# The head of a hybrid decoder step: TensorE's order written out tile by tile, one Newton chain, first weights in three pieces, and a constant table loaded last

## The chip, the cores and the metric

One Trainium2 chip, of which the kernel uses one core. The core has five engines that run their own instruction streams side by side: TensorE (PE in the profile, with its weight loads as PEld), VectorE (DVE), ScalarE (ACT), GpSimd (POOL) and SyncE (SP, which only issues transfers here). Transfers between the chip's memory (HBM) and the on-chip memory (SBUF) run on 16 DMA engines. The metric is the device time of one execution in microseconds, the median of several runs.

## The reference

One inference step of a decoder layer with two branches. The part that the change touches is the layer's beginning, for 1024 prompt tokens and 8 x 4 sample tokens (1056 rows in all, model width 1024):

```
mod = silu(c) @ w_ada + b_ada                 # c: 1 prompt and 8 sample vectors
shift, scale, gate = split(mod, 3)
r = rsqrt(mean(x * x) + EPS)
h = x * r * g_norm * (1 + scale) + shift
u = h @ w_in                                  # then split into queries, keys, values, gates, index rows
...
s = einsum(q_idx, k_idx); relu; weighted sum  # index scores, causal mask, top 256 keys per token
```

After it come the index scores and the choice of 256 keys, sparse attention over the chosen keys, a retention (linear attention) branch, gates, two output projections, a final projection and a norm. None of that is changed.

## The kernel before

Everything in this text happens in the **head**, the first 60 us. `h` is held turned, as eight tiles `k = 0..7` of 128 model channels by 1056 tokens.

- **x blocks** (`x_block`). The x rows are loaded in nine blocks (32 sample rows, then eight blocks of 128 prompt rows). TensorE turns each block into PSUM, ScalarE and VectorE each copy half of it to `XT`, and one of them sums the squares of the rows (VectorE for the blocks listed in `SQD`).
- **Norms** (`norms`). VectorE computes 1/sqrt by Newton steps (`rsqrt`), TensorE spreads the factors over 128 partitions, and a copy leaves them in `RB`.
- **Modulation** (`modulation`). For each `k`, TensorE multiplies the conditioning vectors `scT` with two 512 KB column blocks of `w_ada` (line 212), ScalarE copies the result (`ar`), TensorE turns it, and VectorE reduces it to `cm`, which holds shift and scale of the 128 channels.
- **Tile** (`h_tile`). ScalarE forms the factors `AA` and `BB` (lines 337 and 338), VectorE scales the tile (line 340) and applies the sample rows' own factors (lines 342, 345, 346), ScalarE writes the rounded high part `hh` in two halves (line 348), VectorE the remainder `hl` in two halves (line 349).
- **First products** (`start_two`). The first two 128-column blocks of `w_in` are split into high and low parts `W` and multiplied with all tiles: for each `k` three terms (high weights x `hh`, high x `hl`, low x `hh`), each of five matmuls of 352 or 400 columns, 120 in all, at line 235.

Two more things matter. `C` is a table of constants: its first 128 columns (the identity) are loaded first of all, and the other 664 columns, with a causal mask from column `C_CAUS` on, in one transfer at line 362. The mask is first read by two small VectorE instructions of the index stage, which fill the first blocks of the selection mask `bi`:

```
for b in (0, 1):
    nc.vector.tensor_scalar(BI[b][:, b * 128:], C[:, C_CAUS:C_CAUS + 128], 1.0e30 / 3.0e38, None, op0=OP.mult)
```

They stand far down in the source, but nothing that they need comes from the stages between.

**What sets the order.** Each engine executes its instructions in one fixed order. A scheduler sets that order when the kernel is built, by a timeline of its own; `tc.issue_after(x)` keeps an instruction behind `x`, and `tc.high_priority()` prefers what is inside. So instructions of a later stage can land between those of the head, as the two `bi` instructions do. SyncE issues the loads in its own order, and they are served on one queue.

The functions that the change touches, with the line numbers of the profile:

Of the kernel before, what the change touches and what calls it, by code (L numbers as in the profile page):

```python
# [8 lines left out]
F32 = mybir.dt.float32  # L9
# [4 lines left out]
OP = mybir.AluOpType  # L14
# [4 lines left out]
D = 1024  # L19
# [10 lines left out]
EPS = 1e-6  # L30
SQD = (1, 4)
SEQ = (8, 0, 1, 2, 3, 4, 5, 6, 7)
# [85 lines left out]
def _hybrid_step(ctx, tc, A, outs, dbg):  # L118
# [11 lines left out]
    ps1 = ExitStack()  # L130
    ps = ps1.enter_context(tc.tile_pool(name="ps", bufs=1, reuse_waits="tile", space=PSUM))
    psj_ = ExitStack()
# [92 lines left out]

    def start_two(W):

        x, y = pl(), pl()
        parts_ = [(p[:, :sl.stop - sl.start], sl, i) for p, sl, i in
                  zip((pj(), pj(), x[:, :512], x[:, 512:], y[:, :512]), chunks + late, (0, 0, 0, 1, 1))]  # L230

        line = [(0, 0), (0, 1), (1, 0), (1, 1), (0, 2), (1, 2)] + [(k, term) for k in range(2, KT) for term in range(3)]
        for n, (k, term) in enumerate(line):
            for p, sl, i in parts_:
                nc.tensor.matmul(p, W[i][term == 2][:, k], (HL if term == 1 else HH)[k][:, sl],
                                 start=(n == 0), stop=(n == len(line) - 1))
        return [p for p, sl, i in parts_]

    scT = cst.tile([128, KT, 32], F32, name="scT")
    xp, xs = A["x_prompt"][0], A["x_sample"].rearrange("b i d -> (b i) d")  # L240
    with ExitStack() as s0:
# [5 lines left out]
        part = lambda: sp.tile([128, D], F32, name="x", bufs=11)  # L247
        craw, th = [part()[:9] for _ in (0, 1)]
        nc.scalar.dma_start(craw[0:1], A["c_prompt"])
        nc.scalar.dma_start(craw[1:9], A["c_sample"])  # L250
        rows = sp.tile([48, 128], F32, name="rows")
# [17 lines left out]
        def cond():  # L269
            nc.scalar.activation(th, craw, AF.Tanh, scale=0.5)  # L270
            nc.vector.scalar_tensor_tensor(th, th, 1.0, craw, op0=OP.add, op1=OP.mult)
            pc = pt()
            for k in range(KT):
                nc.tensor.transpose(pc[:, k * 16:k * 16 + 9], th[:, k * 128:k * 128 + 128], ident[:9, :9])
            nc.vector.memset(scT, 0.0)
            nc.scalar.activation(scT[:, :, :9], pc[:, :KT * 16].rearrange("p (k c) -> p k c", c=16)[:, :, :9],
                                 AF.Copy, scale=0.5)
# [7 lines left out]
        def x_block(i):  # L285

            t = SEQ[i]
            n, x = size(t), X[t]
            p = pl().rearrange("p (k t) -> p k t", k=KT)
            for k in range(KT):  # L290
                nc.tensor.transpose(p[:, k, :n], x[:n, 128 * k:128 * k + 128], ident[:n, :n])
# [6 lines left out]
            for g, copy in ((slice(0, 4), nc.scalar.copy), (slice(4, 8), nc.vector.tensor_copy)):  # L298
                copy(XT[:, g, t * 128:t * 128 + n], p[:, g, :n])

        def norms(i0, i1):

            with tc.high_priority():
                v = sp.tile([128, i1 - i0], F32, name="vv", bufs=2)
                nc.vector.tensor_scalar(v, ssq[:, i0:i1], 1.0 / D, EPS, op0=OP.mult, op1=OP.add)
                r = rsqrt(sp, v, i1 - i0)
                newton = nc.cur_bb.bb.instructions[-1]
                p, c0 = pj(), 128 * SEQ[i1 - 4]
                for i in range(i1 - 4, i1):
                    o = 128 * (i - i1 + 4)  # L310
                    last = nc.tensor.matmul(p[:, o:o + 128], r[:, i - i0:i - i0 + 1].to_broadcast([128, 128]), ident, start=True, stop=True)
                nc.scalar.copy(RB[:, c0:c0 + 512], p)
            if i0 == 0:
                p = pt()
                nc.tensor.matmul(p[:, :NS], r[:NS, 0:1].to_broadcast([NS, 128]), ident[:NS, :NS], start=True, stop=True)
                nc.vector.tensor_tensor(XT[:, :, T:], XT[:, :, T:], p[:, :NS].unsqueeze(1).to_broadcast([128, KT, NS]), op=OP.mult)
            return last.ins, newton

        def modulation(k):

            pm = pt()
            for o in (0, 1):
                ada_rows(pm[:, 128 * o:128 * o + 128], lambda c: wa[k][o][:, c])
            ar = sp.tile([128, 256], F32, name="ar", bufs=2)
            nc.scalar.copy(ar, pm[:, :256])
            pm = pt()
            for o in (0, 1):
                turned = nc.tensor.transpose(pm[:, 128 * o:128 * o + 128], ar[:, 128 * o:128 * o + 128], ident)

            cm = sp.tile([128, 2, 9], F32, name="cm", bufs=2)  # L330
            nc.vector.tensor_reduce(cm, pm[:, :256].rearrange("p (o q r) -> p o r q", o=2, q=4)[:, :, :9], op=OP.add, axis=AX.X)
            return cm.rearrange("p o r -> p (o r)"), turned.ins

        def h_tile(k, pm):
# [4 lines left out]
            h = XT[:, k]  # L339
            scaled = nc.vector.scalar_tensor_tensor(h[:, :T], h[:, :T], AA[:, k, 0:1], RB[:, :T], op0=OP.mult, op1=OP.mult)  # L340

# [4 lines left out]
            nc.vector.tensor_tensor(hs, hs, by_seq(BB), op=OP.add)  # L346
            for sl in (slice(0, 528), slice(528, TT)):
                high = nc.scalar.activation(HH[k][:, sl], h[:, sl], AF.Identity, bias=shift)
                rest = nc.vector.scalar_tensor_tensor(HL[k][:, sl], h[:, sl], shift, f32(HH[k][:, sl]), op0=OP.add, op1=OP.subtract)
            return high, rest, moved, scaled  # L350

        wa, loads = {}, []

        def load_wa(k):

            wa[k] = [part().rearrange("p (k f) -> p k f", f=128) for _ in (0, 1)]
            for o, w in enumerate(wa[k]):
                loads.append(nc.sync.dma_start(w, wcols(A["w_ada"][0], KT, 1024 * o + 128 * k, 128)))

        for t in SEQ:  # L360
            x_load(t)
        nc.sync.dma_start(C[:, C_CAUS:], A["cst"][:, C_CAUS:])
# [6 lines left out]
        W, ws = [], []  # L369
        zeros = sp.tile([128, 512], BF, name="zeros")  # L370
        nc.vector.memset(zeros, 0.0)

        def idle_products(n, behind):

            x = pl()
            with tc.issue_after(behind):
                for i in range(n):
                    nc.tensor.matmul(x[:, 512 * (i % 2):512 * (i % 2) + 512], zeros[:, :128], zeros, start=True, stop=True)

        W = [[sp.tile([128, KT, 128], F32R, name="w", bufs=4) for _ in "hl"] for _ in (0, 1)]  # L380
        rounded, rest = lambda i: nc.scalar.copy(W[i][0], ws[i]), lambda i: nc.vector.tensor_sub(W[i][1], ws[i], f32(W[i][0]))
        ends = []
        load_wa(0)
        for k in range(KT):
            if k + 1 < KT:
                load_wa(k + 1)
            if k == 0:
                with tc.issue_after(loads[-1].ins):
                    ws = [wload(wp, w_in, f, 128) for f in (O_KI, O_QI)]
                pm, turned = modulation(k)  # L390
                idle_products(8, turned)
            else:
                with tc.issue_after(spread):
                    pm, turned = modulation(k)
            ends.append(h_tile(k, pm))
            if k == 0:
                for i in (0, 1):
                    with tc.issue_after(ends[0][0 if i else 2].ins):
                        rounded(i)
            if k == 1:  # L400
                for i in (0, 1):
                    with tc.issue_after(ends[1][1 if i else 3].ins):
                        rest(i)
        head_ends = ends[-1]
        first = start_two(W)


# [1107 lines left out]
```

## Time and profile before

| what | value |
|---|---|
| median of 3 runs | 1106.63 us (1106.52 to 1106.79) |
| the profiled execution's own time | 1106.86 us |
| span of its instructions | 1105.1 us |
| granted TensorE clock | 0.998 |
| busy over the span | PE 98%, DVE 61%, ACT 43%, POOL 21% |
| first product of the head (line 235) | starts at 27.04 us |
| last product of the head | starts within the group at 60.28 us; TensorE goes on to line 773 at 60.62 us |

In a row of the timeline the first number is the start in us from the span's beginning, the second the duration, then engine, line, operation, output <- inputs with shapes, the count, and in brackets how long the engine sat idle before it and what ended that. A row of stages gives busy us of each engine and its instructions, the granted clock, the mean busy share of the 16 DMA engines and GB/s.

### The profile page before, as it was taken

To read this page: it belongs to the slowest core of one execution; us is meant where nothing else is said; L and a number is where in the kernel's file an instruction comes from. 1 tells how busy PE (TensorE), PEld (TensorE's weight loads), DVE (VectorE), ACT (ScalarE), POOL (GpSimd) and SP (SyncE) were. 2 spreads that over 40 slices of the span, in tenths; PEclk is the share of its full clock that TensorE was granted. 3 is DMA by queue.
4 is the path that set the end of the run, shared out by engine and by line. 5 is a ranking of instruction groups with operands and counts; after the bars stand their busy time and mean duration, and the time that the engine had idled before them with its cause. 6 is when DMAs were issued, how large, how long until landed. Compare 5 with 4: busy or idle time off the path is not lost. (4 is left out here: it accounts for less than half of the span.)

```text
span 1105.1 us, 20498 instructions
## 1 busy us (share of the span) xinstructions
PE 1078.5 (98%) x8138; PEld 982.2 (89%) x8138; DVE 679.3 (61%) x1646; ACT 471.8 (43%) x916; POOL 229.5 (21%) x195
## 2 busy tenths in 40 slices
PE   6999999999999999999999999999999999999997
PEld 5789899899999989999899999887998888898776
DVE  6876359698877878999122222210357767497765
ACT  6574445554654555332243333311336666343211
POOL 0003016013311221020422222244114333100000
PEclk9999999999999999999999999999999999999999
DMA  9923334264244515532877768486798520367431
GB/s 312 244 72 106 114 110 144 56 212 136 79 144 132 168 42 187 150 87 96 286 246 231 232 186 234 131 285 237 243 326 300 176 75 30 120 201 255 157 120 58
DMA packets 156023, 185.63 MB, mean 168 GB/s; under 512 B 18629, under 2 KB 126989, under 8 KB 154838
## 3 DMA queue, kind: packets, MB, share of 16 engines
q1 hardware_dynamic: 145632, 147.80, 42.7%
q0 software_dynamic: 9856, 35.66, 9.8%
q8 instruction: 64, 1.05, 0.4%
q10 hardware_dynamic: 438, 0.86, 0.2%
q14 instruction: 33, 0.27, 0.1%
HBM read 139.33 MB, written 41.17 MB: 163 GB/s over the span
## 5 line engine op out<-in xcount | busy, mean ns | idle before, releaser
L218 PE MATMUL pj<-hh,wh 128*128 128x352 f32 (+1 forms) x1168 | 383.5, 328 | 1.0 <-ACT raw L720 0.8
L219 PE MATMUL pj<-hl,wh 128*128 128x352 f32 (+1 forms) x1168 | 378.8, 324 | 0.0
L220 PE MATMUL pj<-hh,wl 128*128 128x352 f32 (+1 forms) x1168 | 377.4, 323 | 0.0
L218 PEld LDWEIGHTS pj<-hh,wh 128*128 128x128 f32 x1168 | 219.3, 188 | 10.5 <-issue 7.5
L219 PEld LDWEIGHTS pj<-hl,wh 128*128 128x128 f32 x1168 | 219.7, 188 | 5.0 <-issue 4.4
L220 PEld LDWEIGHTS pj<-hh,wl 128*128 128x128 f32 x1168 | 219.5, 188 | 3.5 <-issue 3.2
L882 DVE TENSOR_SCALAR_CACHE_REDUCE eq<-sc,cand 128x896 bf16<-128x896 f32 (+4 forms) x155 | 135.7, 875 | 2.5
L204 ACT CAST wh<-ws 128x1024 fp32r<-128x1024 f32 (+1 forms) x65 | 61.0, 942 | 111.4 <-PE pj L219 82.3
L205 DVE TENSOR_TENSOR wl<-ws,wh 128x1024 fp32r<-128x1024 f32 (+1 forms) x47 | 52.6, 1122 | 35.7 <-ACT wh L204 35.4
L205 POOL TENSOR_TENSOR wl<-ws,wh 128x1024 fp32r<-128x1024 f32 x18 | 43.1, 2394 | 147.6 <-ACT wh L204 147.6
L1229 POOL TENSOR_SCALAR lg<-lg,st 128x1024 f32<-128x1024 f32 (+7 forms) x64 | 47.6, 752 | 115.5 <-DVE st L1228 58.7
L1099 DVE COPY kt<-str 128x512 f32<-128x512 f32 x32 | 22.1, 690 | 64.3 <-PE str L1097 60.6
L1227 ACT ACTIVATE lg<-lg,st 128x1024 f32<-128x1024 f32 (+7 forms) x64 | 49.4, 774 | 27.6 <-DVE st L1226 26.0
L1426 PE MATMUL pj<-woh,MH 128*128 128x512 f32 (+1 forms) x136 | 51.4, 378 | 0.0
L1427 PE MATMUL pj<-wol,MH 128*128 128x512 f32 (+1 forms) x136 | 51.2, 377 | 0.0
L1428 PE MATMUL pj<-woh,ML 128*128 128x512 f32 (+1 forms) x136 | 51.2, 376 | 0.0
L1066 POOL DMA_INDIRECT kv<-in_cache_k,idx x32 | 30.1, 940 | 93.1 <-PE str L1097 83.6
L720 ACT ACTIVATE raw<-pj 128x352 f32<-128x352 f32 x48 | 22.1, 463 | 53.0 <-PE pj L220 46.1
L1242 PE MATMUL tr<-C,lg 128*128 128x128 f32 x288 | 43.0, 278 | 1.5 <-ACT pT L1245 0.6
L1066 POOL DMA_INDIRECT kv<-in_cache_v,idx x32 | 30.6, 957 | 54.3 <-PE sx L1127 27.9
L1099 ACT COPY kt<-str 128x512 f32<-128x512 f32 x32 | 18.8, 588 | 52.1 <-PE str L1097 40.8
L1242 PEld LDWEIGHTS tr<-C,lg 128*128 128x128 f32 x288 | 32.5, 140 | 9.1 <-issue 4.9
(351 smaller groups left out, 1969.0 us busy)
## 6 DMA issues: line engine op xcount, KB each, us to landing
ws<-in_w_in SPq DMA_DIRECT2D x51, 512.0 KB
rot<-in_rot SPq DMA_DIRECT2D x8, 1056.0 KB
x<-in_w_ada SPq DMA_DIRECT2D x16, 512.0 KB
TG<-raw SPq DMA_DIRECT2D x15, 528.0 KB
wst<-in_w_out SPq DMA_DIRECT2D x12, 512.0 KB
u<-TG SPq DMA_DIRECT2D x8, 528.0 KB
t<-TG SPq DMA_DIRECT2D x8, 528.0 KB
x<-in_x_prompt SPq DMA_DIRECT2D x8, 512.0 KB
```

The lines of the kernel that those rows point to most:

```text
L204: nc.scalar.copy(wh[:, :, :n], ws[:, :, :n])
L205: (nc.vector if k == 4 or len(order) % 3 else nc.gpsimd).tensor_sub(wl[:, :, :n], ws[:, :, :n], f32(wh[:, :, :n]))
L218: nc.tensor.matmul(p, wh[:, k], HH[k][:, sl], start=(k == 0), stop=False)
L219: nc.tensor.matmul(p, wh[:, k], HL[k][:, sl], start=False, stop=False)
L220: nc.tensor.matmul(p, wl[:, k], HH[k][:, sl], start=False, stop=(k == KT - 1))
L882: nc.vector.tensor_scalar(junk[:n, :W], sc, thr[:n, j:j + 1], 0.0, op0=op, op1=OP.add, accum_out=cnt[:n, j:j + 1])
L1066: nc.gpsimd.indirect_dma_start(out=t.rearrange("p s c -> p (s c)"), out_offset=None, in_=cache.rearrange("g (r s) h d -> (g r) (s h d)", s ...
L1227: nc.scalar.activation(l, l, AF.Exp, bias=st[:, 2:3], scale=0.125, accum_out=st[:, 3:4])
L1242: step["turned"] = nc.tensor.transpose(x[:, 128 * (j - j0):128 * (j - j0) + 128], lg[:, j % 2, 128 * (j // 2):128 * (j // 2) + 128], ident)
L1426: nc.tensor.matmul(x, MH[:, k, tk], wh[:, k], start=(k == 0), stop=False)
L1427: nc.tensor.matmul(x, MH[:, k, tk], wl[:, k], start=False, stop=False)
L1428: nc.tensor.matmul(x, ML[:, k, tk], wh[:, k], start=False, stop=(k == KT - 1))
```

## The change

Only the head is changed; from the index products on (line 791) every engine executes the same rows in the same order as before.

- x blocks are turned into single PSUM banks (four buffers `px`) instead of double ones (two buffers `pl`); VectorE takes four sums of squares instead of two; the condition vectors are handled as 72 rows of 128 instead of 9 rows of 1024.
- One Newton chain for all nine blocks instead of one for five and one for four.
- TensorE's order is written out for every tile: `modulate(k)`, `turn`, and `products` of one tile and term at a time (`put`, `take`, `set_out`). Four instead of eight idle products.
- The first two blocks of `w_in` are loaded in three pieces (2, 2 and 4 of 8 row blocks), between the `w_ada` loads, and split piece by piece (`high`, `low`).
- The 664 columns of `C` are loaded behind all `w_ada` blocks instead of ahead of them.

The core of the diff:

```diff
-SQD = (1, 4)
+SQD = (0, 2, 4, 7)
...
         for t in SEQ:
             x_load(t)
-        nc.sync.dma_start(C[:, C_CAUS:], A["cst"][:, C_CAUS:])
+        ws = [wp.tile([128, KT, 128], F32, name="ws", bufs=2) for _ in (0, 1)]
+        pieces = (slice(0, 2), slice(2, 4), slice(4, 8))
...
+        load_wa(0)
+        load_wa(1)
+        first_weights(pieces[0])
+        for k in range(2, KT):
+            load_wa(k)
+            if k in (2, 4):
+                first_weights(pieces[k // 2])
+        with tc.issue_after(loads[-1].ins):
+            nc.sync.dma_start(C[:, C_CAUS:], A["cst"][:, C_CAUS:])
         cond()
         for i in range(9):
-            x_block(i)
-            if i == 4:
-                norms(0, 5)
-        spread, newton = norms(5, 9)
+            held = x_block(i, i == 8)
+        with tc.high_priority():
+            ar, multiplied = modulate(0, last_on(mybir.EngineType.PE))
+        spread, newton, pm = norms(lambda behind: turn(ar, behind))
...
+        take(1)
         for k in range(KT):
...
+            if k == 0:
+                set_out(1)
+            ends.append(h_tile(k, turned.pop(k)))
...
+            put(k, 0)
+            put(k, 1)
+            take(k + 2)
+            if k > 0:
+                if k == 1:
+                    put(0, 2)
+                put(k, 2)
+            if k + 2 < KT:
+                set_out(k + 2)
-        first = start_two(W)
+        first = [p for p, sl, i in banks]
```

`put(k, term)` issues the five products of one tile and term, `take(k)` the modulation products of tile `k`, `set_out(k)` their turning; each is kept behind the one before it.

What this does to the loads on SyncE. Before, in the order of issue (`C` 128x664 is the table, `ws` the weight blocks):

```order
L267 DMA x<-in_x_prompt 128x1024 x8
L362 DMA C<-in_cst 128x664
L358 DMA x<-in_w_ada 128x8x128 x4
L198 DMA ws<-in_w_in 128x8x128 x2
L358 DMA x<-in_w_ada 128x8x128 x12
```

After:

```order
L265 DMA x<-in_x_prompt 128x1024 x8
L375 DMA x<-in_w_ada 128x8x128 x4
L387 DMA ws<-in_w_in 128x2x128 x2
L375 DMA x<-in_w_ada 128x8x128 x2
L387 DMA ws<-in_w_in 128x2x128 x2
L375 DMA x<-in_w_ada 128x8x128 x4
L387 DMA ws<-in_w_in 128x4x128 x2
L375 DMA x<-in_w_ada 128x8x128 x6
L397 DMA C<-in_cst 128x664
```

The table moved from ahead of the first of 18 blocks of 512 KB (16 of `w_ada`, two of `w_in`) to behind the last; the `w_in` blocks are cut in pieces.

On VectorE, the readers of the table (`bi0`, `bi1`) stood before among the last x blocks, between steps of the first Newton chain (`rs_t`, `rs_y`):

```order
L299 COPY xt_120<-pl_246 128x4x128
L173 SCALAR_TENSOR_TENSOR rs_t_225<-rs_y_224 128x5
L942 TENSOR_SCALAR bi0_94<-C_75 128x128
L942 TENSOR_SCALAR bi1_95<-C_75 128x128
L174 TENSOR_TENSOR rs_t_225<-rs_t_225,vv_222 128x5
L305 TENSOR_SCALAR vv_294<-ssq_107 128x4
```

After, they stand behind the last remainder of tile 3 (`hl3`) and ahead of the scaling of tile 4 (line 352):

```order
L362 SCALAR_TENSOR_TENSOR hl3_88<-xt_118,BB_121,hh3_80 128x512
L342 TENSOR_REDUCE cm_561<-pt_558 128x18
L362 SCALAR_TENSOR_TENSOR hl3_88<-xt_118,BB_121,hh3_80 128x544
L1015 TENSOR_SCALAR bi0_94<-C_75 128x128
L1015 TENSOR_SCALAR bi1_95<-C_75 128x128
L352 SCALAR_TENSOR_TENSOR xt_118<-xt_118,AA_120,rb_119 128x1024
L357 TENSOR_TENSOR xt_118<-xt_118,AA_120 128x32
L428 TENSOR_TENSOR w_371<-ws_140,w_370 128x512
L354 TENSOR_SCALAR BB_121<-cm_561,cols_117,BB_121 128x8
L362 SCALAR_TENSOR_TENSOR hl4_89<-xt_118,BB_121,hh4_81 128x512
```

The two readers moved from the x blocks to the middle of the eight tiles; all of VectorE's work for tiles 4 to 7 now stands behind them.

On TensorE the stretch around tile 4 was before a mixture of tiles (`hh4` is high part of tile 4, `w_317` and `w_319` high weights, `w_318` and `w_320` low, `pt` the modulation):

```order
L235 MATMUL pl_643<-hh3_80,w_319 128x400
L235 MATMUL pj_644<-hh4_81,w_317 128x352
L235 MATMUL pj_645<-hl3_88,w_317 128x352
L235 MATMUL pl_642<-hl3_88,w_317 128x352
```

After, tile 3 ends with its low-weight term and the turning of tile 5's modulation, and tile 4 follows:

```order
L212 MATMUL pt_585<-x_170,scT_103 32x128 x8
L234 MATMUL pj_418<-hh3_80,w_371 128x352
L234 MATMUL pj_419<-hh3_80,w_371 128x352
L234 MATMUL pl_416<-hh3_80,w_371 128x352
L234 MATMUL pl_416<-hh3_80,w_373 128x400
L234 MATMUL pl_417<-hh3_80,w_373 128x400
L339 MATMUL pt_609<-C_75,ar_602 128x128 x2
L234 MATMUL pj_418<-hh4_81,w_370 128x352
```

The first product of tile 4 now closes TensorE's stream to everything behind it, the modulation of tiles 6 and 7 among it.

More of the change, by code (lines that the diff above doesn't have):

```diff
@@ L309, in norms @@
[L309 to L316, printed above, removed]
@@ L317, in norms @@
-            return last.ins, newton
-        def modulation(k):
+                spread = None
+                for g, copy in enumerate((nc.scalar.copy, nc.vector.tensor_copy)):
+                    p = pj()
+                    with tc.issue_after(turned.ins if g else multiplied):
+                        for o in range(4):
+                            i = 1 + 4 * g + o
+                            spread = nc.tensor.matmul(p[:, 128 * o:128 * o + 128], r[:, i:i + 1].to_broadcast([128, 128]), ident, start=True, stop=True).ins
+                    copy(RB[:, 512 * g:512 * g + 512], p)
+                    if g == 0:
+                        pm, turned = turn(spread)
@@ L321, in modulation, with modulate @@
+            p = pt()
+            with tc.issue_after(spread):
+                spread = nc.tensor.matmul(p[:, :NS], r[:NS, 0:1].to_broadcast([NS, 128]), ident[:NS, :NS], start=True, stop=True).ins
+            nc.vector.tensor_tensor(XT[:, :, T:], XT[:, :, T:], p[:, :NS].unsqueeze(1).to_broadcast([128, KT, NS]), op=OP.mult)
+            return spread, newton, pm
+        def modulate(k, behind):
             pm = pt()
[L322 to L323 removed]
+            with tc.issue_after(behind):
+                for o in (0, 1):
+                    ada_rows(pm[:, 128 * o:128 * o + 128], wa[k][o])
+            last = last_on(mybir.EngineType.PE)
@@ L377, in idle_products @@
                 for i in range(n):
-                    nc.tensor.matmul(x[:, 512 * (i % 2):512 * (i % 2) + 512], zeros[:, :128], zeros, start=True, stop=True)
+                    last = nc.tensor.matmul(x[:, 512 * (i % 2):512 * (i % 2) + 512], zeros[:, :128], zeros, start=True, stop=True)
+            return last.ins
         W = [[sp.tile([128, KT, 128], F32R, name="w", bufs=4) for _ in "hl"] for _ in (0, 1)]
-        rounded, rest = lambda i: nc.scalar.copy(W[i][0], ws[i]), lambda i: nc.vector.tensor_sub(W[i][1], ws[i], f32(W[i][0]))
@@ L382, in _hybrid_step, with high, low, put @@
-        ends = []
-        load_wa(0)
+        def high(i, g, behind):
+            with tc.issue_after(behind):
+                nc.scalar.copy(W[i][0][:, g], ws[i][:, g])
+        def low(i, g, behind):
+            with tc.issue_after(behind):
+                nc.vector.tensor_sub(W[i][1][:, g], ws[i][:, g], f32(W[i][0][:, g]))
+        behind = idle_products(4, spread)
+        ends, banks, turned = [], None, {0: pm}
+        def put(k, term):
+            nonlocal behind
+            with tc.issue_after(behind):
+                behind = products(W, banks, k, term)
@@ L384, in _hybrid_step, with take, set_out @@
+        def take(k):
+            nonlocal behind
+            if k < KT:
+                with tc.issue_after(ends[k - 2][0].ins if k > 1 else behind):
+                    turned[k], behind = modulate(k, behind)
+        def set_out(k):
+            nonlocal behind
+            if k < KT:
+                turned[k], t = turn(turned[k], behind)
+                behind = t.ins
+        take(1)
         for k in range(KT):
-            if k + 1 < KT:
-                load_wa(k + 1)
             if k == 0:
[L388 to L394, printed above, removed]
@@ L401, in _hybrid_step @@
+            if k in (1, 2, 4):
                 for i in (0, 1):
-                    with tc.issue_after(ends[1][1 if i else 3].ins):
-                        rest(i)
+                    low(i, pieces[(1, 2, 4).index(k)], ends[k][1 if k > 1 and i else 3].ins)
+            put(k, 0)
[7 more added lines that the diff above has]
+                set_out(k + 2)
```

95 lines of the change are left out of this document (55 added, 40 removed).

## The prediction

> **What bounds the kernel now.** I read the page first, for the engine that carries the span, then the head in stages, then its timeline engine by engine.
>
> ```profile
> PE 1078.5 (98%) x8138; PEld 982.2 (89%) x8138; DVE 679.3 (61%) x1646; ACT 471.8 (43%) x916; POOL 229.5 (21%) x195
> ```
>
> TensorE is busy for nearly the whole span, so time gained or lost in the head passes on to the end: behind the head all engines run the same rows in the same order, and their loads hang on events of the head and shift with them. The stages of the head:
>
> ```profile
> 5.00:10.00 5.00, 4.33 (x25) 3.97 (x25) 2.82 (x5) 3.75 (x8) 0.00 (x0) 1.00 1.02 405
> 25.00:30.00 5.00, 3.17 (x43) 2.26 (x36) 2.51 (x5) 4.09 (x7) 0.00 (x0) 1.00 0.97 274
> 30.00:35.00 5.00, 3.46 (x57) 2.18 (x57) 4.34 (x9) 2.53 (x6) 0.00 (x0) 1.00 1.17 295
> 45.00:50.00 5.00, 5.00 (x59) 4.33 (x62) 4.62 (x13) 3.23 (x6) 0.00 (x0) 1.00 1.09 295
> 50.00:55.00 5.00, 5.00 (x51) 4.76 (x40) 4.09 (x9) 2.36 (x6) 0.00 (x0) 1.00 0.13 38
> 55.00:60.00 5.00, 5.00 (x32) 5.00 (x31) 3.60 (x7) 3.65 (x7) 0.85 (x1) 1.00 0.00 0
> ```
>
> The next to last number is the busy share of the DMA engines: they are full from 5 to 50 us and empty behind. The 512 KB blocks come at some 295 GB/s. TensorE (first pair) has gaps until 35 us and none later. So the head is bound by the loads in its first half and by the work on the eight tiles in its second.
>
> Which loads land when is read where TensorE waits for them:
>
> ```profile
> 33.96 0.64 PE L212 MATMUL pt<-x,scT 128*32 128x128 f32 x16 [1.07 <-DMA x<-in_w_ada]
> 41.27 0.64 PE L212 MATMUL pt<-x,scT 128*32 128x128 f32 x16 [0.54 <-DMA x<-in_w_ada]
> 43.66 0.60 PE L212 MATMUL pt<-x,scT 128*32 128x128 f32 x13 [0.30 <-DMA x<-in_w_ada]
> ```
>
> In the order of issue these are blocks 10, 14 and 15 of the 18 that precede the end of the `w_ada` loads (tile 3's second half, tile 5's second half, tile 6's first). From 10 to 14: 7.31 us over four blocks, 1.83 us each.
>
> **What decides the change: the table at the end of the queue.** `C`'s 664 columns and their readers before:
>
> ```profile
> 7.41 0.43 SPq L362 DMA_DIRECT2D C<-in_cst  x1
> 16.73 0.16 DVE L173 SCALAR_TENSOR_TENSOR rs_t<-rs_y 128x5 f32<-128x5 f32 x1
> 16.80 0.35 DVE L942 TENSOR_SCALAR bi<-C 128x128 bf16<-128x128 f32 x2
> 17.07 0.16 DVE L174 TENSOR_TENSOR rs_t<-rs_t,vv 128x5 f32<-128x5 f32 x1
> ```
>
> The table was there, and the two readers cost 0.35 us without any wait. Now it is served behind all 18 blocks, which need the same bytes ahead as the last block does today. That block lands at 41.27 + 4 x 1.83 = 48.6 us, or counted from block 15 at 43.66 + 3 x 1.83 = 49.2. With the table's 332 KB moved from ahead of the blocks to behind them, the sum of bytes up to its own landing is the same, so **the table lands at about 48.6 us**.
>
> Its readers now stand in VectorE's order between tile 3's last remainder and tile 4's scaling. At today's pace VectorE would be there before 43.91 us, where tile 4's scaling starts today (row below). So VectorE stands for some 5 us or more, and behind it stands all its work on tiles 4 to 7; TensorE has nothing but tile 3's products and tile 5's modulation left, and then stops at the first product of tile 4. Does an engine really let ready work stand behind a waiting instruction? Today's profile shows it on ScalarE:
>
> ```profile
> 24.61 0.18 DVE L345 TENSOR_TENSOR xt<-xt,AA 128x32 f32<-128x32 f32 x1
> 25.30 1.04 ACT L381 CAST w<-ws 128x1024 fp32r<-128x1024 f32 x1 [1.75 <-DMA ws<-in_w_in]
> 26.25 1.36 ACT L348 ACTIVATE hh<-xt,BB 128x528 fp32r<-128x528 f32 x2
> 27.04 0.43 PE L235 MATMUL pj<-hh,w 128*128 128x352 f32 x1 [1.63 <-ACT hh L348]
> ```
>
> The high part of tile 0 could have started at 24.79, when the scaling and line 345 were done; it starts at 26.25, behind a cast that waited for its load, and TensorE waits for it.
>
> **From the table's landing to the end of the head.** The pace of one tile, from today's tile 6 to the end of the head:
>
> ```profile
> 43.91 1.27 DVE L340 SCALAR_TENSOR_TENSOR xt<-xt,AA,rb 128x1024 f32<-128x1024 f32 x1
> ...
> 51.10 1.28 DVE L340 SCALAR_TENSOR_TENSOR xt<-xt,AA,rb 128x1024 f32<-128x1024 f32 x1
> 52.30 0.18 DVE L345 TENSOR_TENSOR xt<-xt,AA 128x32 f32<-128x32 f32 x1
> 52.41 0.28 DVE L342 TENSOR_SCALAR BB<-cm,cols,BB 128x8 f32<-128x8 f32 x1
> 52.72 0.19 DVE L346 TENSOR_TENSOR xt<-xt,BB 128x32 f32<-128x32 f32 x1
> 53.25 0.77 DVE L349 SCALAR_TENSOR_TENSOR hl<-xt,BB,hh 128x528 fp32r<-128x528 f32 x1 [0.34 <-ACT hh L348]
> 54.56 0.23 DVE L331 TENSOR_REDUCE cm<-pt 128x18 f32<-128x72 f32 x1 [0.54 <-PE pt L328]
> 54.71 0.76 DVE L349 SCALAR_TENSOR_TENSOR hl<-xt,BB,hh 128x528 fp32r<-128x528 f32 x1
> 55.38 1.28 DVE L340 SCALAR_TENSOR_TENSOR xt<-xt,AA,rb 128x1024 f32<-128x1024 f32 x1
> ```
> ```profile
> 60.28 0.68 PE L235 MATMUL pl<-hh,w 128*128 128x352 f32 x3
> 60.62 0.32 PEld L773 LDWEIGHTS pt<-C,kiT 128*128 128x128 f32 x2
> ```
> ```profile
> L348 ACT ACTIVATE hh<-xt,BB 128x528 fp32r<-128x528 f32 x14 | 9.9, 732 | 8.1 <-DVE xt L345 6.9 <-DVE xt L346 1.2
> L337 ACT ACTIVATE AA<-cm,cols 128x9 f32<-128x9 f32 x7 | 2.7, 390 | 1.5 <-DVE cm L331 1.4
> L381 DVE TENSOR_TENSOR w<-ws,w 128x1024 fp32r<-128x1024 f32 x2 | 2.4, 1217 | 0.0
> L325 ACT COPY ar<-pt 128x256 f32<-128x256 f32 x6 | 2.2, 370 | 4.4 <-PE pt L212 4.4
> ```
>
> (The last four: mean ns of one behind the bar.) Worked along the new order, from the landing:
> - the two readers, 0.35;
> - tile 4, **5.2**: scaling and line 345 1.3, a low weight piece of 512 columns 0.6 (half of 1217 ns), line 342 0.3, remainder 0.7, line 346 0.2; only then can ScalarE write the second high half, 0.75; second remainder 0.75 and a second low piece 0.6;
> - tile 5, **3.9**: scaling 1.3, first high half 0.75, remainder 0.7; on ScalarE the copy of tile 6's modulation, 0.37, comes ahead of the second half, 0.75, whose remainder ends the step;
> - tile 6, **4.3**: today's step, 55.38 - 51.10, with the same members: turning of tile 7's modulation, reduction 0.23, factors 0.39;
> - tile 7 to the end of the products, **5.24**: 60.62 - 55.38.
>
> Sum 19.0 us; the head would end at 48.6 + 19.0 = 67.6 instead of 60.62, **+7.0 us**.
>
> TensorE stands for about 6 us: today it reaches tile 4 near 45 us, and now its first product needs the readers, the scaling and a high half behind the table, 48.6 + 0.35 + 1.3 + 0.75 = 51.0. What a rested TensorE does shows at the start, while the granted clock in the stage 5 to 10 us reads 1.00:
>
> ```profile
> L291 PEld LDWEIGHTS pl<-C,x x14: 180/230/230, 5.8 to 8.4; 128*128 128x128 f32 x14
> ...
> L291 PEld LDWEIGHTS pl<-C,x x16: 139/141/143, 14.1 to 15.7; 128*128 128x128 f32 x16
> ```
>
> The same weight loads take 230 ns in the first 3 us of work and 141 later, a factor of 1.63. Bounds for tile 4: nothing, if only the program's start is slow or VectorE's chain hides it, and 3 x (1 - 1/1.63) = 1.2 us, if a pause does the same and all of it lies on the path. Tile 6's reduction waits on TensorE just where these products stand, so I take a little over the middle, **+0.7 us**. [...]
>
> **The rest of the change costs and gains nothing while this wait stands.** Fixed tile order, one Newton chain, single banks, the moved sums of squares, shorter condition rows, four idle products fewer and the earlier first weight piece all act before tile 4. If they bring the first product from 27.04 forward, TensorE only reaches the wait sooner; if one Newton chain makes it later, by up to the 5 us of the wait, nothing is lost. Their cover is the wait itself: with it gone they would count in full. The prefetch of the next two weight blocks shares its buffers with the pieces, so it waits for VectorE's low pieces at tile 4 and is issued at about 51 and 54 us, 8 us later than today:
>
> ```profile
> 43.40 4.08 SPq L198 DMA_DIRECT2D ws<-in_w_in  x2
> 58.03 1.99 ACT L204 CAST wh<-ws 128x1024 fp32r<-128x1024 f32 x2
> ```
>
> At 1.83 us a block on an otherwise empty queue both are there before their casts, which move with the head's end to about 65 us. POOL's order is unchanged.
>
> Sum: +7.0 + 0.7 = +7.7 us. Against the profiled execution, 1106.86 (a span of 1105.1 and 1.8 around it), that is 1114.6; its time is 0.2 above the median, so on the median 1106.63 + 7.7 = **1114.3 us**, slower by 0.7%. A change within 0.2% (2.2 us) counts as none.
>
> **Rivals.**
> - *VectorE catches up.* The work for tiles 4 to 7 is partly ready by then, and if VectorE never waits for ScalarE or TensorE, its own busy time decides: 4 x (1.20 + 0.11 + 0.31 + 0.12 + 0.15 + 2 x 0.69) = 13.1, plus 0.35 and two low pieces 1.2, 14.6 us; the last ten products take 10 x 0.16 (31 in the 5 us from 55 to 60), 1.6. End 64.8, +4.2: 1110.8. For it: DVE is the fullest engine of the stages from 30 to 50 us. Against it: tile 7's modulation stands on TensorE behind products that need tile 5's remainder. Chance 0.13.
> - *No wait (the other side).* Should VectorE reach the readers only when the table is there, above 48.6, or the scheduler's order not hold, tiles 4 to 7 follow at once. The first weight piece lands three quarters of a block and the table's 0.8 us earlier than today's 25.30, at about 23.1 (332 KB at 405 GB/s are 0.8); with a cast and a matmul's start behind it the first product could come at 23.6, 3.4 us earlier, and with no later wait in its place that gives 1106.6 - 3.4 = 1103.2. It decides if the readers start within a fraction of a us of tile 3's end. Against it: the 5 us between. Chance 0.03.
> - *No wait and no gain.* Without the readers' wait, tile 1's turned modulation, which now stands ahead of the first product and behind ScalarE's casts, keeps the start near 27 us: 1106.4. Chance 0.04.
> - *A later table and a slow TensorE.* Landing at 49.5, +0.9, and the slow products on the path in full, 1.2 instead of 0.7: +9.1, 1115.7. Chance 0.07.
>
> My forecast has the rest, 0.73. The range takes in the catching-up case and the last one with as much again above it as a slower step of one tile would give: 1110.6 to 1116.4; it leaves out the two cases without a wait and what the steps miss, under 2 in 10. Slower has 0.93, same 0.04, faster 0.03.
>
> **What would show it.** In the changed kernel's timeline the `bi<-C` pair on VectorE starts at 48 to 50 us with 4 to 8 us idle before it, released by the transfer of `in_cst`; behind it scaling of tile 4; TensorE's first product of `hh4` near 51 us with about 6 us idle; the last product of line 234 at 67 to 69 us; the stages behind the head as today, shifted. The forecast is wrong if the table lands before 45 us, if the pair shows no wait, or if tiles 4 to 7 take less than 17 us.

## The result and the profile after

| kernel | median | runs | ratio to before, 95% interval |
|---|---|---|---|
| before, same chip | 1106.58 us | 1105.97 to 1106.79 (4) | 1 |
| after | 1115.32 us | 1114.01 to 1117.50 (4) | 1.0082 [1.0064, 1.0099] |
| after, a second time | 1115.87 us | 1111.96 to 1118.86 (6) | 1.0088 [1.0070, 1.0106], against 1105.89 |

The change costs 8.7 us, beyond the 0.2% that counts as none. The profiled execution took 1117.5 us (span 1115.7, granted clock 0.991).

First the place on which the prediction rests. VectorE's timeline of after, the readers of the table and the scaling of the tiles:

```profile
39.09 1.28 DVE L352 SCALAR_TENSOR_TENSOR xt<-xt,AA,rb 128x1024 f32<-128x1024 f32 x1 [0.46 <-ACT AA L348]
...
47.87 0.36 DVE L1015 TENSOR_SCALAR bi<-C 128x128 bf16<-128x128 f32 x2 [4.56 <-DMA C<-in_cst]
48.15 1.28 DVE L352 SCALAR_TENSOR_TENSOR xt<-xt,AA,rb 128x1024 f32<-128x1024 f32 x1
...
53.25 1.28 DVE L352 SCALAR_TENSOR_TENSOR xt<-xt,AA,rb 128x1024 f32<-128x1024 f32 x1
...
57.44 0.23 DVE L342 TENSOR_REDUCE cm<-pt 128x18 f32<-128x72 f32 x1 [1.30 <-PE pt L339]
...
58.28 1.28 DVE L352 SCALAR_TENSOR_TENSOR xt<-xt,AA,rb 128x1024 f32<-128x1024 f32 x1
...
62.50 1.28 DVE L352 SCALAR_TENSOR_TENSOR xt<-xt,AA,rb 128x1024 f32<-128x1024 f32 x1 [0.46 <-ACT AA L348]
```

The readers stand 4.56 us, released by the transfer of the table, and tile 4's scaling stands behind them: between the scaling of tiles 3 and 4 lie 9.1 us. TensorE at the same time, and the head's end (the first product with `kiT`) after and before:

```profile
45.70 0.69 PE L234 MATMUL pl<-hh,w 128*128 128x352 f32 x3
50.56 0.69 PE L339 MATMUL pt<-C,ar 128*128 128x128 f32 x2 [4.16 <-ACT ar L331]
50.90 0.64 PE L234 MATMUL pj<-hh,w 128*128 128x352 f32 x1
...
67.81 0.44 PE L846 MATMUL pt<-C,kiT 128*128 128x128 f32 x2
```
```profile
60.80 0.38 PE L773 MATMUL pt<-C,kiT 128*128 128x128 f32 x2
```

The head ends 7.0 us later by these two rows (the prediction counted from the weight load at 60.62; all head ends below are starts of this product). The stages of after, with the granted clock third from the end of a row, and the weight loads of line 234 behind the rest and later (min, median, max ns, and from when to when):

```profile
45.00:50.00 5.00, 1.40 (x20) 0.86 (x9) 2.13 (x5) 0.48 (x1) 0.00 (x0) 0.82 0.36 107
50.00:55.00 5.00, 4.02 (x12) 3.24 (x12) 4.38 (x11) 2.09 (x6) 0.00 (x0) 0.50 0.47 115
55.00:60.00 5.00, 4.99 (x77) 4.12 (x80) 3.35 (x8) 2.29 (x6) 0.00 (x0) 1.00 0.37 95
```
```profile
L234 PEld LDWEIGHTS pl<-hh,w x3: 330/330/333, 52.1 to 52.7; 128*128 128x128 f32 x3
```
```profile
L234 PEld LDWEIGHTS pl<-hh,w x6: 187/188/192, 56.3 to 57.7; 128*128 128x128 f32 x6
```

A weight load behind the rest takes 330 ns, later 188, a factor of 1.76. Read in steps of 0.5 us, the granted clock is 0.50 from 48.2 to 55.0 us: it falls 1.8 us into the rest and stays down for 4.4 us behind it. In the second profile of the same kernel the rest is 4.40 us, and the clock is down from 51.7 to 58.6 us (0.68 over the stage 50 to 55, 0.64 over 55 to 60), all of it behind the rest. So nearly the same rest costs a different amount from one execution to the next.

The head is not all. The same two VectorE instructions (the causal add of an index block, and the mean of a retention stage), before and then after:

```profile
110.61 0.29 DVE L801 TENSOR_TENSOR sc<-sc,C 128x128 f32<-128x128 f32 x1
...
410.79 1.35 DVE L691 TENSOR_REDUCE mu<-O 128x18 f32<-128x1152 f32 x1 [2.73 <-ACT O L680]
```
```profile
116.07 0.29 DVE L874 TENSOR_TENSOR sc<-sc,C 128x128 f32<-128x128 f32 x1
...
421.14 1.35 DVE L764 TENSOR_REDUCE mu<-O 128x18 f32<-128x1152 f32 x1 [2.73 <-ACT O L753]
```

After is 7.0 us late at the head's end, 5.46 at 116 us, and 10.35 at 421 us. So 1.5 us come back soon behind the head, and 4.9 us are lost in a place that the change does not touch. There TensorE waits twice (its timeline of after), and its clock falls (stages of after, then of before; the same time of the clock is some 5 us further on in the work of before):

```profile
401.07 1.15 PE L689 MATMUL pt<-vtok,kd 128*64 128x64 f32 x32 [0.78 <-ACT kd L667]
403.40 1.97 PE L701 MATMUL pb<-qrT,krT 64*64 64x128 f32 x16 [1.18 <-DVE tmp L707]
```
```profile
400.00:405.00 5.00, 3.05 (x50) 2.58 (x48) 4.96 (x12) 1.17 (x4) 2.29 (x1) 0.81 0.29 86
405.00:410.00 5.00, 5.00 (x20) 4.71 (x17) 1.39 (x2) 2.27 (x2) 0.00 (x0) 0.50 0.10 25
```
```profile
400.00:405.00 5.00, 5.00 (x58) 4.67 (x57) 3.60 (x10) 4.63 (x8) 0.00 (x0) 1.00 0.05 10
```

Before has the same two groups at 394.70 and 396.01 us, with 0.16 us of waiting in all and the clock at 1.00. So the two waits make 1.8 us of the loss, and the other 3.1 come with the slow clock behind them (0.50 over the stage 405 to 410). VectorE is full in this stretch after (4.96 of 5 us), and the loss is not made up: the profiled execution ends 10.6 us later than that of before (1117.50 against 1106.86).

### The profile page after: what moved, and what is told of

The parts are those of the page before. It is cut to its first block, busy times and chain, and to the rows that moved or that the text cites. A ratio compares the mean times of both kernels' runs of the same rounds, so it can differ in the third digit from the quotient of the medians.

```text
span 1115.7 us, 20469 instructions
## 1 busy us (share of the span) xinstructions
PE 1083.9 (97%) x8126; PEld 987.2 (88%) x8127; DVE 685.0 (61%) x1644; ACT 468.5 (42%) x915; POOL 230.1 (21%) x195
## 5 line engine op out<-in xcount | busy, mean ns | idle before, releaser
L1302 POOL TENSOR_SCALAR lg<-lg,st 128x1024 f32<-128x1024 f32 (+7 forms) x64 | 48.2, 759 | 115.0 <-DVE st L1301 57.8
```

## The experiments

The 13 profiles beside that of before in one table: head end; how much later than before the two VectorE instructions of the last fences are; and the medians.

| kernel | head end | at 110.6 | at 410.8 | median (n) | ratio, 95% |
|---|---|---|---|---|---|
| after | 67.81 | +5.46 | +10.35 | 1115.32 (4) | 1.0082 [1.0064, 1.0099] |
| after_again | 69.76 | +7.40 | +9.07 | 1115.87 (6) | 1.0088 [1.0070, 1.0106] |
| e1_table_first | 63.95 | +1.62 | +6.65 | 1110.01 (8) | 1.0028 [1.0014, 1.0042] |
| e2_readers_behind | 62.32 | -0.02 | -0.02 | 1108.61 (12) | 1.0029 [1.0015, 1.0043] |
| e3_busy_wait | 68.53 | +6.18 | +6.19 | 1112.62 (5) | 1.0062 [1.0049, 1.0075] |
| e4_only_table_last | 61.28 | -0.64 | -0.58 | 1105.99 (11) | 0.9997 [0.9988, 1.0006] |
| e5_wait_alone | 66.13 | +4.20 | +4.27 | 1109.27 (7) | 1.0030 [1.0019, 1.0041] |
| e6_warm_spread | 61.36 | -1.00 | -0.94 | 1105.53 (11) | 1.0003 [0.9992, 1.0015] |
| e7_whole_weights | 61.38 | -0.99 | +1.42 | 1106.86 (12) | 1.0013 [1.0000, 1.0026] |
| e8_own_scratch | 60.41 | -1.94 | +0.04 | 1106.42 (11) | 0.9998 [0.9989, 1.0007] |
| e9_work_into_wait | 67.27 | +4.92 | +10.15 | 1115.71 (5) | 1.0081 [1.0067, 1.0094] |
| e10_shifted_code | 60.51 | -1.86 | -1.79 | 1107.43 (11) | 1.0010 [1.0001, 1.0019] |
| e11_after_shifted | 68.10 | +5.75 | +5.76 | 1112.78 (5) | 1.0060 [1.0046, 1.0074] |

The ratio goes by the runs of before beside which a kernel was timed (medians 1105.89 to 1106.58). A profile is one execution; the median is over all.

`after_again` is the changed kernel a second time, to see whether the pause at 400 us stands in every execution. Expected were 1112 to 1117 us with a median near 1115 and, in some executions, no pause. The pause stands in this profile too (0.62 and 1.18 us), but the clock stays at 1.00 behind it, and 1.7 us are lost in place of 4.9. Its head ends 2.0 us later than after's: the readers start 0.6 us later, and the step from tile 5 to 6 takes 1.3 us more under a slow clock that lasts longer.

**e1: after, with the table ahead of the tiles' blocks again.**

```diff
+        loads.append(nc.sync.dma_start(C[:, C_CAUS:], A["cst"][:, C_CAUS:]))
         load_wa(0)
...
-        with tc.issue_after(loads[-1].ins):
-            nc.sync.dma_start(C[:, C_CAUS:], A["cst"][:, C_CAUS:])
```

> The changed kernel with one line moved back: the 664 columns of the table are loaded ahead of the first w_ada block again, all else as changed. Main theory (the loss is VectorE's wait for the table and what TensorE's rest costs behind it): tile 4's scaling follows tile 3's last remainder at once, near 44 us (0.8 later than it could, since the table's bytes stand ahead of the blocks again) instead of 48.15; the granted clock stays 1.00 behind 35 us; the head ends at 61 to 63 us instead of 67.8; time 1106 to 1109. Rival (another part of the change, the fixed order or the one Newton chain, is as dear): head end above 65, time above 1112.

**e2: after, the table last, but its readers behind the head.**

```diff
-            nc.vector.tensor_scalar(BI[b][:, b * 128:], ...)
+            with tc.issue_after(head_ends[1].ins):
+                nc.vector.tensor_scalar(BI[b][:, b * 128:], ...)
```

> The changed kernel with the table loaded last as changed, but its two readers on VectorE kept behind the last tile of the head. Main theory: what costs is not that the table comes late but that ready work stands behind its readers. Then tile 4's scaling starts near 43.3 us, the readers run without a wait near 60, the head ends at 60 to 62 us, time 1105 to 1108, 0 to 1 us below the run with the table first. Rival (the late table itself costs, by the queue or by the loads behind it): within 1 us of the changed kernel.

Both take the wait away in a different manner, and the head's end falls by 3.9 and 5.5 us (67.81 to 63.95 and 62.32), the medians by 5.3 and 6.7. Both stay a little above what was expected, in head end and time, and below their rivals. The readers of e2, with no wait:

```profile
60.52 0.35 DVE L1016 TENSOR_SCALAR bi<-C 128x128 bf16<-128x128 f32 x2
```

So the wait is the main cost. But neither comes down to before: 1.5 us are left at e2's head end (62.32 against 60.80). Loading the table last is no loss in itself: e2's head ends 1.6 us earlier than e1's, with Newton chains that agree within 0.1 us (one profile of each).

**e3: after, with 18 products of zeros (512 columns each) in TensorE's rest.**

```diff
+            if k == 3:
+                behind = idle_rows(18, behind)
```

> The changed kernel with 18 products of zeros on TensorE in the time in which it stands (behind tile 3's last product, ahead of the turning of tile 5's modulation), to keep it busy; nothing else is changed, their results are not used. The prediction's clock term: with TensorE busy up to tile 4 the weight loads of tile 4 take 188 ns instead of 330, the granted clock in 50 to 55 us is 1.00 instead of 0.50, VectorE's wait of 1.30 us for tile 6's modulation is gone, and the head ends 0.7 to 1.3 us earlier, at 66.5 to 67.1. Rival (the slow clock lies beside VectorE's chain): clock 1.00, head end unchanged within 0.2.

The clock stays up:

```profile
45.00:50.00 5.00, 4.95 (x52) 2.94 (x52) 1.29 (x3) 0.00 (x0) 0.00 (x0) 1.00 0.43 124
50.00:55.00 5.00, 3.97 (x34) 2.60 (x36) 3.72 (x10) 2.31 (x5) 0.00 (x0) 1.00 0.41 105
```

From the readers' start to the head's end it is 19.82 us, in after 19.94, so as a remedy it brought nothing, as the rival had it. The steps between the scalings tell why: 5.79, 4.23, 4.23 and 5.30 us, where after has 5.10, 5.03, 4.22 and 5.31. The step from tile 5 to tile 6, which waits for TensorE, is 0.8 shorter at full clock. But the scheduler set VectorE's reduction for tile 5 later (54.09 in place of 51.28), which costs 0.7. In after_again, whose clock is down until 58.6 us, that step is 6.35; in e2, without the rest, 3.75. Against e2 the slow clock is worth 1.3 and 2.6 us in this step, against e3, with its other order, 0.8 and 2.1. No run takes the slow clock away and leaves the order as it is.

**e4: before, with only the table last.**

```diff
-        nc.sync.dma_start(C[:, C_CAUS:], A["cst"][:, C_CAUS:])
...
+            if k + 2 == KT:
+                with tc.issue_after(loads[-1].ins):
+                    nc.sync.dma_start(C[:, C_CAUS:], A["cst"][:, C_CAUS:])
```

> The kernel before with one part of the change: the table loaded behind the w_ada blocks. The scheduler puts the two readers elsewhere here, on VectorE ahead of the reduction of tile 6, which starts at 49.6 us in the kernel before. Main theory (the price is set by where the readers stand against the landing at 47.9 to 48.6): no wait above 0.3 us, head end 60 to 61, time 1105.5 to 1107. Rival (a late table costs wherever its readers stand): 3 us or more above the kernel before.

```profile
43.86 1.28 DVE L340 SCALAR_TENSOR_TENSOR xt<-xt,AA,rb 128x1024 f32<-128x1024 f32 x1
46.03 1.28 DVE L340 SCALAR_TENSOR_TENSOR xt<-xt,AA,rb 128x1024 f32<-128x1024 f32 x1
49.06 0.36 DVE L944 TENSOR_SCALAR bi<-C 128x128 bf16<-128x128 f32 x2 [0.67 <-DMA C<-in_cst]
```

The same late table costs nothing where the scheduler puts the readers two tiles further back: 0.67 us of waiting, ratio 0.9997. The price is set by where the readers stand, not by the load.

**e5: before, with the wait alone.** The table last, and the readers put ahead of the scaling of tiles 4 to 7:

```diff
+            if k == 4:
+                with tc.issue_after(ends[3][1].ins):
+                    reader = ...                  # the two bi instructions
+            with tc.issue_after(reader.ins if k > 3 else spread):
+                ends.append(h_tile(k, pm))
```

> The kernel before with only the wait added: table C behind the 18 blocks, and its two readers put on VectorE behind tile 3's last remainder and ahead of the scaling of tiles 4 to 7. Theory (the readers' wait is the price, whatever the rest of the order): the readers start at 48.5 to 49.5 us after 4 to 6 us of waiting, tile 4's scaling right behind them, and the head ends where the 17.4 us that ran from tile 4's scaling (43.86) to the head's end (61.28) with the table last and unread lead to: 49.4 + 17.4 = 66.8, say 65 to 67 (before: 60.62). Time 1110 to 1112.5. Rival (the wait costs so much only together with the fixed order of TensorE, because there nothing can run ahead): head end below 63, time below 1108.5.

```profile
49.98 0.36 DVE L401 TENSOR_SCALAR bi<-C 128x128 bf16<-128x128 f32 x2 [4.41 <-DMA C<-in_cst]
50.26 1.28 DVE L340 SCALAR_TENSOR_TENSOR xt<-xt,AA,rb 128x1024 f32<-128x1024 f32 x1
51.75 1.27 DVE L340 SCALAR_TENSOR_TENSOR xt<-xt,AA,rb 128x1024 f32<-128x1024 f32 x1
```

The head ends at 66.13, +5.3 us: as much as e2 took away. The time, 1109.27, is 0.7 below what was expected: 1.1 us come back by 110 us, and the median is another 1.4 us below the profiled execution (1110.68), which stays open. Here two tiles are scaled back to back behind the wait, because tile 5's rows were turned in time; from the readers on it is 16.15 us, in after 19.94. VectorE is busy 15.3 and 15.5 us of that, so after's order has the same work and 3.6 us more of gaps. Two things differ, and no run takes them apart: the strict order of TensorE and ScalarE, in which tile 5's rows stand behind tile 4's high part, and a longer slow clock (0.83 over this stretch, 0.89 in e5).

**e9: after, with the last low halves of the weights taken up in tile 3's turn**, so that they run in VectorE's wait:

```diff
-            if k in (1, 2, 4):
+            if k in (1, 2, 3):
                 for i in (0, 1):
-                    low(i, pieces[(1, 2, 4).index(k)], ...)
+                    low(i, pieces[k - 1], ...)
```

> The changed kernel with the last third of the low halves of the first weights (two VectorE instructions of some 0.69 us, L428) taken up in tile 3's turn, so that they run in VectorE's wait and not behind the readers; ScalarE's copy of tile 5's rows then stands ahead of tile 4's high part too. Theory (the readers' wait costs by the work that VectorE has still to do behind it): two L428 ahead of the readers, the wait 3.0 to 3.5 us in place of 4.56, head end 1.2 to 2.0 us nearer to the readers (18.0 to 18.7 us from the readers' start, 19.94 before), time 1 to 2 us below after's in a median over scattered runs. Rival (behind the wait TensorE at half clock sets the steps): 19.5 us or more from readers to head end, time as after's.

The wait is 1.49 us (this execution's Newton chain was late, too), and from readers to head end it is 18.93 in place of 19.94: 1.0 us, less than the 1.2 to 2.0 expected. The step from tile 4 to 5 fell from 5.10 to 3.49, and the next rose from 5.03 to 5.62 at a clock of 0.66, with TensorE now last. In the medians nothing is seen; this profile loses 5.2 us between 110 and 411 us.

**e6: e2, with eight products of zeros behind tile 0's modulation.** What is left of the change without the wait?

```diff
             ar, multiplied = modulate(0, last_on(mybir.EngineType.PE))
+            multiplied = idle_rows(8, multiplied)
```

> The kernel of e2_readers_behind with eight products of zeros put on TensorE between tile 0's modulation and the spreading of the norms, to fill the rest of 1.88 us behind the Newton chain. Theory (the one Newton chain makes TensorE rest and its clock falls; the slow spreading and turning behind it are what the rest of the change costs): granted clock 1.00 from 20 to 30 us, 16 spreading products in some 2.2 us in place of 3.5, first products at 27.5 to 28.5 in place of 29.7, head end 60.3 to 61.2 in place of 62.3, time 1.3 to 2 us below e2's, 1106.5 to 1107.3. Rival (VectorE's and ScalarE's chain of scaling, high parts and remainders sets the head, the clock only beside it): head end 62 to 62.5, time as e2's, 1108.6.

TensorE spreads the norms behind the one Newton chain, in e2 and in e6, with the stage of each:

```profile
21.66 1.58 PE L313 MATMUL pj<-C,rs_y 128*128 128x128 f32 x8 [1.88 <-DVE rs_y L175]
...
23.46 1.91 PE L313 MATMUL pj<-C,rs_y 128*128 128x128 f32 x8
```
```profile
20.00:25.00 5.00, 3.34 (x18) 3.34 (x18) 2.79 (x11) 1.69 (x5) 0.00 (x0) 0.72 1.19 307
```
```profile
21.51 1.16 PE L313 MATMUL pj<-C,rs_y 128*128 128x128 f32 x8
...
22.72 1.06 PE L313 MATMUL pj<-C,rs_y 128*128 128x128 f32 x8
```
```profile
20.00:25.00 5.00, 4.00 (x27) 2.90 (x26) 3.43 (x13) 2.00 (x6) 0.00 (x0) 1.00 1.19 307
```

Clock 1.00, head end 61.36, 1.0 us earlier, with a Newton chain that ended only 0.15 us earlier: the direction held, the gain was just short of the 1.1 to 2.0 us expected. The median fell by 3.1 us, more than the head accounts for; both kernels scatter widely and were timed on different chips. The execution's own luck counts as much as the clock: in the profiles with this one chain and the shared scratch, the chain's last instruction starts between 20.2 and 21.6 us.

**e7: e2, with each first weight in one piece.**

```diff
-        first_weights(pieces[0])
+        first_weights(slice(0, 8))
         for k in range(2, KT):
             load_wa(k)
-            if k in (2, 4):
-                first_weights(pieces[k // 2])
```

> The kernel of e2_readers_behind with each first weight loaded in one piece of 512 KB again, behind the blocks of tiles 0 and 1, in place of three pieces. Theory (the pieces are hidden, they cost and bring nothing): head end 62 to 62.8, time within 1 us of e2's 1108.6, and runs as scattered as e2's (1106.1 to 1114.8). Rival A (the pieces bring the later blocks early): head end 63.5 or more. Rival B (the four transfers more on SyncE's queue are what lets a later stage slip): the scatter goes, every run within 2 us of the fastest.

Head end 61.38, below the 62 to 62.8 expected, with a Newton chain that ended 1.15 us earlier than e2's: the pieces bring and cost nothing that can be told here. The scatter stays (1105.71 to 1113.14), so it does not come from the four transfers more.

**e8: e6, with VectorE's squares off the shared scratch.**

```diff
-            sq = BI[7]
+            sq = RB.bitcast(BF)[:, :D] if t in SQD else BI[7]
```

and four products of zeros in place of eight.

> The kernel of e6_warm_spread with four products of zeros in place of eight, and VectorE's squares written to the not yet used rows RB in place of the scratch BI[7] that they share with ScalarE's: in e2 VectorE's last square stood 0.99 us until ScalarE's was out of it. Theory (the Newton chain starts when the last square is done, and what follows it goes on from there): VectorE's last square with no wait, the chain's end 0.8 to 1.2 us earlier (20.2 to 20.6 us in place of 21.4), head end 60.2 to 60.8 in place of 61.36, time 1103.8 to 1105.2 against 1105.53. Rival (tile 0's weights, which land at 19 us, or the transfers behind them hold the head): head end 61.2 or more, time as e6's. This one may beat both kernels.

VectorE's last square (line 290) starts in e2 at 17.91 us, 0.99 us idle before it, released by ScalarE's square into the same scratch (line 293); in e8 it starts at 16.20 with no idle time. The wait is gone, and the head ends at 60.41, 0.4 us earlier than in before; the time stays above what was expected (median 1106.42), and in the profile, whose time is the median, 2.0 us are lost again between 110 and 411 us.

**e10 and e11: e8 and after, with twelve tiny products of zeros where TensorE waits anyway.** They are there to move the place at which TensorE's code is loaded (by the reading below). Where does the late loss begin? On SyncE's queue after, in the four issues that swap halves of the retention's key rows:

```profile
363.12 0.58 SPq L651 DMA_DIRECT2D tmp<-krT  x1
363.75 1.36 SPq L650 DMA_DIRECT2D tmp<-krT  x1
365.16 0.59 SPq L651 DMA_DIRECT2D tmp<-krT  x1
```

One takes 1.36 us in place of 0.58. The page's list of queues has, over the whole span:

```profile
q8 instruction: 64, 1.05, 0.4%
```

64 loads of 16 KB; TensorE's 8126 matmuls and 8127 weight loads make 254 for each, which points to TensorE's code: the author's reading, since no view names the engine that a load is for. One of them starts at 363.5 to 363.7, right when the slow issue begins. In the time of before (less the offset at 110 us) this load starts (read in windows of 0.25 us), and the slowest of the four issues takes:

| kernel | load starts | slowest issue | lost from 110 to 411 us |
|---|---|---|---|
| after, after_again, e1, e7, e9 | 358.0 to 358.25 | 1.31 to 1.86 us | 1.7 to 5.2 us |
| e8 | 357.5 | 1.40 us | 2.0 us |
| before, e3, e4, e5, e6 | 355.0 to 356.75 | 0.58 to 0.59 us | 0.0 to 0.1 us |
| e2 | 359.0 | 0.59 us | 0.0 us |

After has some 23 TensorE instructions fewer than before (8126 and 8127 against 8138 and 8138), and the load falls some 2 us later in the work, on these issues. With the 24 instructions more of e10 and e11 it falls 1.8 and 2 us earlier again.

```diff
+        x = pt()
+        with tc.issue_after(spread):
+            for i in range(12):
+                spread = nc.tensor.matmul(x[:, :32], zeros[:, :128], zeros[:, :32], start=True, stop=True).ins
         behind = idle_products(4, spread)
```

> The changed kernel with the same twelve tiny products, nothing else. Theory: the head as in after (readers near 48, head end 67.5 to 70), but no slow krT issue and no loss at 400 us: the offset to the kernel before stays what it is at 100 us, 5.5 to 7.4, so 1112 to 1113.8 in the median in place of 1115.9, and the runs within 3 us. Rival (the late loss is the head's or chance): 1115 to 1116.5, scattered over 5 us or more as before.

The issue in e11, where the load starts near 356.1 in the time of before:

```profile
364.04 0.58 SPq L654 DMA_DIRECT2D tmp<-krT  x1
```

The offset stays at 5.75 until 411 us, and the median falls to 1112.78 (1111.93 to 1114.68), with a head as late as after's. So some 2.5 to 3 us of the change's 8.7 are likely this; the kernels were timed on different chips, and their intervals overlap a little.

How the slow issue leads to the waits 35 us later is not shown. GpSimd's first work on the swapped rows starts 1.1 us late in after, beyond the offset, but also 1.0 us late in e2, whose load falls into the fourth issue; there every issue takes its usual time, and nothing is lost by 411 us.

> The kernel of e8_own_scratch with twelve tiny products of zeros (32 columns each, 24 instructions with their weight loads) on TensorE behind the spreading, where it waits more than a us for VectorE. They do nothing but move the place at which TensorE's next block of instructions is loaded. In the profiles so far one transfer on the instruction queue q8 starts, counted in the time of the kernel before, at 358.0 to 358.25 us in after, after_again, e1, e7 and e9, at 357.5 in e8, and there one of SyncE's four issues of row copies takes 1.3 to 1.9 us in place of 0.58 and the run is 1.7 to 5.2 us later behind 400 us; at 355.0 to 356.75 in before, e3, e5 and e6, and at 359.0 in e2, and there neither is seen. Theory (that load in the way of that issue is the late loss): with 24 instructions more it comes near 355.7, every krT issue is 0.55 to 0.6 us, the gain of 1.94 us against before that e8 had until 370 us is kept to the end, time 1104.0 to 1105.2, and the runs lie within 2 us. Rival (chance, or the head's shift, makes the late loss): the issue is slow in half of the executions still, time as e8's, 1106.4.

The profile did as expected: load near 355.6, no slow issue, a gain of 1.86 us at 110 us and 1.79 at 411, 1104.19 us. The median did not: 1107.43, scattered from 1104.19 to 1110.37. That is no better than e8's median, as the rival had it, so the late load explains the profiles, not all of the scatter. What strikes the other runs stays open, and with it the scatter of e2 and e7.

No version here beats before by what a measurement can tell (e8: 0.9998 [0.9989, 1.0007]; e6: 1.0003 [0.9992, 1.0015]). Both beat the changed kernel by 0.8%.

## Why the prediction was right

Right in total (1114.3 against 1115.32, in the range) and in its mechanism: the readers' wait for the late table, with the work of tiles 4 to 7 behind it. That the total came so close is in part luck, since two errors behind the head partly cancel, and the head itself was 7.0 us late in one profile and 9.0 in the other, with 7.7 forecast.

- *The table lands at about 48.6*: 47.87 and 48.50 in two executions. Right.
- *VectorE stands some 5 us or more*: 4.56 and 4.79, a little less. Shown as the cause by e1, e2 and e5, which take it away or put it in alone.
- *Tile 4, 5.2; tile 6, 4.3; tile 7 to the end, 5.24*: 5.10, 4.22, 5.31.
- *Tile 5, 3.9*: 5.03 and 6.35. Without the rest of TensorE it is 3.75 (e2), so the step was right at full clock, and what is over is the clock's term.
- *The slow clock, +0.7, bounds 0 to 1.2*: 1.3 and 2.6 us. These are against e2; against e3 they are 0.8 and 2.1. The term was mis-sized: its upper bound took 3 us of slow work and a factor of 1.63 from the program's start, and the slow clock lay on 4.4 and 6.9 us behind the rest, with a factor of 1.76. After its first 6 us, TensorE rests in before for at most 1.63 us (ahead of the product at 27.04, with a clock of 1.00 in the stage 25 to 30), so the term was an estimate from the rows at the start alone.
- *TensorE stands about 6 us, its first product of tile 4 at 51*: 4.16 us and 50.90. TensorE came to its stop at 46.4 and not near 45, and the turning of tile 5's rows, ahead of the product, ends the wait 0.3 us sooner.
- *The rest costs and gains nothing while the wait stands; uncovered it counts in full*: uncovered it costs 1.5 us in e2's profile; the first product starts at 29.68, later than the 27.04 of before. About 1 us is the slow clock behind the one Newton chain (e6). The chain itself ends later for the wait on the shared scratch (e8). And while the wait stands the new order is not free either: from the readers to the head's end it needs 19.94 us, the old one in e5 16.15, though there the readers start 2.1 us later.
- *Behind the head all shifts with it*: wrong twice. Up to 116 us 1.5 us come back, as 1.1 to 1.6 do in every variant, e4's too; before's row is below. And at 360 to 410 us up to 5 us are lost, most likely by the shift of TensorE's code, which an order of instructions does not show.
- *Two readings of the stages before* were wrong, and no term of the sum hangs on them. TensorE has gaps after 35 us, too (4.16 us busy from 40 to 45). And VectorE is the fullest engine only from 30 to 35 us; from 35 to 50 it is TensorE (5.00, 4.16 and 5.00 us against 3.60, 3.88 and 4.62), so this reading does not speak for the rival in which VectorE catches up. After, VectorE is busy for 15.5 us of the 19.94 behind the readers and waits in the rest.

```profile
79.02 0.48 PE L791 MATMUL pl<-kih,qs 128*128 128x512 f32 x1 [1.28 <-DVE qs L756]
```

This wait of before, with another of 0.22 us at 72.74, makes the 1.5 us; after has neither. It is not the later head that takes them away: e8's head ends earlier than before's, and 1.55 us come back there too. Between the head and line 791 the order differs: ScalarE's casts for two blocks of queries (`qs<-pj`, at 75.01 us after, at 69.37 before) now stand ahead of two others (`qs<-pl`, at 76.02, before at 68.36). So the premise that all behind the head keeps its order does not hold in this stretch. Whether the order is what removes the wait was not tried.

An estimate of the 8.7 us from these profiles and medians: 5.3 to 5.5 for the readers' wait (e5, e2), 1.5 for the rest of the change, 1.5 given back, some 3 lost late (e11). That makes 8.3 to 8.5.

## What to carry to other kernels

When a load is moved to the end of a queue, look where each of its readers stands in its engine's order, however small and however far down in the source: what decides is the work behind the reader, not the reader. A time saved or lost in one stage need not reach the end, so compare the same instruction at several places of the run, not only the end; here even the place at which code is loaded seems to count. And before a rest on TensorE is called hidden, look at the granted clock behind it: here rests of 4.16 and 4.40 us were followed by 4.4 and 6.9 us at 0.50, which counted on the next step that waits for TensorE, with 0.8 to 2.6 us.

## What the hardware showed that was not expected

- In e2 rests of 0.29, 1.17 and 1.88 us with two groups of 0.64 us between them are followed by a clock of 0.50 from 22.2 to 25.6 us (0.72 over the stage 20 to 25). With the last of them filled (e6) it stays at 1.00.
- In all six profiles in which a 16 KB load on the instruction queue q8 starts at 357.5 to 358.25, one transfer's issue on SyncE takes 1.31 to 1.86 us in place of 0.58; in none of the other eight is one of these four issues slow. How the one holds up the other was not tried.
